# A conditioned decoder layer on one core: a new order for its opening

## The chip, the cores and the metric

The kernel runs on one core of a Trainium2 chip. The core has TensorE (PE, matrix products into PSUM; PEld is its weight load), VectorE (DVE), ScalarE (ACT), GpSimd (POOL) and SyncE (SP). SP, ScalarE and GpSimd each issue transfers, which run on 16 shared DMA engines. The metric is the device time of one execution in microseconds (us); smaller is better.

## The reference

One layer over x of 256 rows by 2048, in f32. A vector c of 2048 conditions it: nine rows of shifts, scales and gates come from `silu(c) @ w_ada + b_ada`.

```
c_act = silu(c)
mod = (c_act @ w_ada + b_ada).reshape(9, 2048)
h = rms_norm(x, norm_ffn1) * (1 + mod[1]) + mod[0]
x = x + 0.5 * mod[2] * swiglu(h, w_ffn1_gu, w_ffn1_down)     # w_gu: 2048 x 11264
h = rms_norm(x, norm_mix) * (1 + mod[4]) + mod[3]
x = x + mod[5] * token_mixing(h)                             # retention and windowed attention
h = rms_norm(x, norm_ffn2) * (1 + mod[7]) + mod[6]
x = x + 0.5 * mod[8] * swiglu(h, w_ffn2_gu, w_ffn2_down)
out = rms_norm(x, norm_final)
```

The change touches the first three lines and the beginning of the first `swiglu`.

## The kernel before

Everything is cut into tiles of 128 partitions. x lies in two row tiles t = 0 and 1 (`x_sb`); the 2048 columns are 16 blocks k of 128. To keep f32 accuracy at the speed of the rounded product type, every operand is split into a rounded part and the rest: ScalarE casts (`wh`, `hh`), VectorE subtracts (`wl`, `hl`), and `products` (lines 320 to 329) makes three matmuls of 512 columns for each k and t: `hh·wh`, `hl·wh`, `hh·wl`.

**The condition.** w_ada comes transposed, one row of 128 x 2048 (1 MB) for each mod index m and block k. `cact` holds silu(c) on every partition: c is loaded as one row (line 146), four matmuls with a column of ones spread it, and ScalarE applies Silu to each quarter (lines 168 to 171). `ada_pass` (line 204) multiplies half a row with half of `cact` and sums along it on VectorE; `ada_end` (221 to 224) adds the two halves and applies bias and gain. The gains and biases are loaded as short rows by `small_loads` (150 to 157, six transfers on SP, the identity among them) and turned into columns by three transposes in `columns_in` (175 to 188).

**The opening.** `place(m, k)` loads a w_ada row. The rows of k = 0 use two of the four `raw` buffers; all later rows take turns on a ring of two halves of one big tile, so the third row on the ring can be loaded only when the first has been passed. x's mean squares are summed on ScalarE in four parts a row tile (line 462, into the two `pd` banks, whose content nobody reads); `inv_rms` (474 to 488) makes 1/rms with a square root on ScalarE and six small VectorE operations. Block k of h is x times 1/rms (787), transposed on TensorE (788), modulated (497), and split (502, 503).

**The first products.** The first 12 column blocks n of w_gu are worked on while the condition is still being made: k comes in groups of 2, 3, 3, 4 and 4 blocks, and for each group all 12 n are visited (`visit`): load the k rows of block n into a `raw`, split, multiply. Between the groups the sums go to SBUF (`to_parts`, lines 835 and 837). During the visits of one group the rows of the next are loaded, passed, and made into h (`group`), a step at a time.

**What sets the order.** On SP the order is the program's, always. On the other engines a planner orders the instructions by its own estimate of when each can start, but for stretches under `manual_schedule(engines=ORDERED)`, where TensorE, VectorE and ScalarE also follow the program. Before the change only the ends of the three long products have such a stretch; the opening is the planner's. A DMA on SP uses one of eight semaphores in turn. In the planner's order, GpSimd's first transfers are the table of cosines and masks (879) and the sinks (880), though the program has them after the first FFN.

The opening's SP order is c, row (1,0), x tile 0, x tile 1, six small loads, row (0,0), rows (1,1) and (0,1), then w_gu blocks.

Of the kernel before, what the change touches and what calls it, by code (L numbers as in the profile page):

```python
# [17 lines left out]
P = 128  # L18
# [59 lines left out]
def layer_kernel(  # L78
# [38 lines left out]
    def nm(s):  # L117
        uid[0] += 1
        return f"{s}_{uid[0]}"
# [30 lines left out]
    def small_loads():  # L150
        nc.sync.dma_start(ident, consts[:, C_ID : C_ID + P])
        for i, src in enumerate((norm_ffn1, norm_mix, norm_ffn2)):
            nc.sync.dma_start(
                rows[i * KD : (i + 1) * KD, :P], src[0].rearrange("(k p) -> k p", p=P)
            )
        nc.sync.dma_start(rows[:, P : 2 * P], b_rows[:P])
        nc.sync.dma_start(rows[: 9 * KD - P, 2 * P : 3 * P], b_rows[P:])
# [10 lines left out]
    for j in range(D // CH):  # L168
        pt = acc_bank()
        nc.tensor.matmul(pt, ones, c_row[:, j * CH : (j + 1) * CH], start=True, stop=True)  # L170
        nc.scalar.activation(cact[:, j * CH : (j + 1) * CH], pt, AF.Silu)
# [108 lines left out]
    def gate_load(row, m):  # L280
        nc.gpsimd.dma_start(row, gate_d[m // 3][None, :].broadcast_to([P, D]))
# [186 lines left out]
    def inv_rms(ssq, t):  # L468
# [6 lines left out]
            out=s, in_=ssq[:, t * 4 : (t + 1) * 4], axis=AX.X, op=ALU.add  # L475
# [15 lines left out]
    def modulated(held, k, src, m_shift, act=False):  # L491

        h = t512()[:, :S]
        scale = modc[:, m_shift + 1, k : k + 1]
        shift = modc[:, m_shift, k : k + 1]
        if act:
            nc.scalar.activation(h, src, AF.Identity, bias=shift, scale=scale)
        else:
            nc.vector.tensor_scalar(
                out=h, in0=src, scalar1=scale, scalar2=shift, op0=ALU.mult, op1=ALU.add  # L500
            )
        nc.scalar.copy(held.hi[:, k, :], h)
        nc.vector.tensor_sub(held.lo[:, k, :], h, held.hi[:, k, :].bitcast(F32))  # L503
# [255 lines left out]

    place(1, 0)  # L760
    for t in range(NT):
        nc.sync.dma_start(x_sb[:, t, :], x[0, t * P : (t + 1) * P, :])
    small_loads()
    place(0, 0)
    place(1, 1)
    place(0, 1)
    columns_in()

    def group(ks):

        for k in ks:
            for m in (1, 0):
# [4 lines left out]
                if ks[0] == 0:  # L777
                    ada_end(m, slice(k, k + 1), early[m], 0 if m else None, passes)
                yield
        if ks[0] > 0:  # L780
            for m in (1, 0):
                ada_end(m, slice(ks[0], ks[-1] + 1), early[m], 0 if m else None, passes)
# [9 lines left out]
    for t in range(NT):  # L792
        for ci in range(4):
            square_sum(
                ssq[:, t * 4 + ci : t * 4 + ci + 1], x_sb[:, t, ci * CH : (ci + 1) * CH]
            )
    r = [inv_rms(ssq, t) for t in range(NT)]
    bounds = (0, 2, 5, 8, 12, 16)
    groups = [range(a, b) for a, b in zip(bounds, bounds[1:])]


    banks, moved = {}, set()
    chunks = list(range(2 * EARLY))

    def load_blocks(n, ks):
        raw = raws.tile([P, KB, CH], F32, tag="raw", name=nm("raw"))
        c0 = (n % 2) * DFF + (n // 2) * CH
        nc.sync.dma_start(
            raw[:, : len(ks), :],
            gu[ks[0] * P : (ks[-1] + 1) * P, c0 : c0 + CH].rearrange("(k p) n -> p k n", p=P),  # L810
        )
        return raw
# [27 lines left out]
    for _ in group(groups[0]):  # L840
        pass
    for g, ks in enumerate(groups):
# [5 lines left out]
        for i, n in enumerate(order):  # L848
            visit(n, ks, load_blocks(n, ks), n not in stay)
# [16 lines left out]
    gate_load(gate, 2)  # L866
# [12 lines left out]
    nc.gpsimd.dma_start(small_c[:, C_COS:], consts[:, C_COS:C_DEC])  # L879
    nc.gpsimd.dma_start(sink_b, sinks.broadcast_to([P, QH]))  # L880
# [369 lines left out]
```

## Time and profile before

| | us |
|---|---|
| median of 3 runs | 2430.84 (2430.41 to 2431.67) |
| profiled execution, first to last instruction | 2429.6 |
| first product of TensorE (spreading c) | 2.60 |
| first pass over a w_ada row | 7.02 |
| first product with w_gu | 26.57 |
| TensorE busy in the whole span | 2385.2 |

The profiled execution's own time is given as its span alone, 2429.6; the median of the runs is 1.2 above it. A row of the timeline reads: start, duration, engine, line of the kernel, operation, tile written <- tiles read, shapes, count, and in brackets the idle time before it with what ended it. An engine name with q (SPq) is its sequencer issuing a transfer. A row of the stage table reads: stretch, length, then busy time and number of instructions for each engine, the granted TensorE clock, the mean busy share of the DMA engines, and GB/s. A transfer's row gives its size and the time from issue to landing. A waits row gives the whole time, the number of times and the longest.

### The profile page before, as it was taken

The page shows a single profiled execution, that of the slowest core. Times are in us where ns is not written, and L with a number is a line of the kernel's source. Part 1 is how long each engine was busy: PE and PEld are TensorE (multiplying, and loading weights), DVE is VectorE, ACT ScalarE, POOL GpSimd, SP SyncE. Part 2 cuts the span into 40 slices and gives each one's busy share as a digit, 9 for nine tenths or more (in the row PEclk, how much of TensorE's full clock was granted, in tenths as well). Part 3 has the DMA queues.
Part 4 walks back from the last instruction along what each step waited for, and adds up shares of the span by engine and source line. Part 5 has one row for each costly group of instructions (what it writes and reads, how often), then busy time and mean ns, then how long its engine had stood idle before and what let it go on. Part 6 is the DMA issues. An engine that isn't in the chain of part 4 may idle for free. (4 is left out here: it accounts for less than half of the span.)

```text
span 2429.6 us, 29064 instructions
## 1 busy us (share of the span) xinstructions
PE 2385.2 (98%) x10798; PEld 1946.8 (80%) x10798; DVE 1701.3 (70%) x2735; ACT 1236.0 (51%) x1696; POOL 5.7 (0%) x14
## 2 busy tenths in 40 slices
PE   7999999999999999999999999999999999999998
PEld 4778888888787777788888888887788888888886
DVE  6998777778877677886666776767655555555656
ACT  6544545454545455554544444446554555554544
POOL 0000000000000000000000000000000000000000
PEclk9999999999999999999999999999999999999999
DMA  9987689998875665566676777755677777775563
GB/s 347 341 333 284 217 313 318 356 319 295 311 264 186 243 222 204 206 219 216 233 266 245 251 260 260 279 189 190 215 249 237 243 251 238 248 237 192 185 198 122
DMA packets 274545, 606.43 MB, mean 250 GB/s; under 512 B 40098, under 2 KB 40482, under 8 KB 255586
## 3 DMA queue, kind: packets, MB, share of 16 engines
q1 hardware_dynamic: 272898, 597.91, 70.8%
q0 software_dynamic: 928, 5.61, 0.6%
q8 instruction: 85, 1.39, 0.2%
q10 hardware_dynamic: 576, 1.05, 0.1%
q14 instruction: 58, 0.47, 0.1%
HBM read 595.06 MB, written 2.12 MB: 246 GB/s over the span
## 5 line engine op out<-in xcount | busy, mean ns | idle before, releaser
L336 DVE TENSOR_TENSOR wl<-raw,wh 128x1024 fp32r<-128x1024 f32 (+1 forms) x828 | 995.9, 1208 | 591.2 <-ACT wh L335 585.3
L335 ACT CAST wh<-raw 128x1024 fp32r<-128x1024 f32 (+1 forms) x828 | 861.4, 1042 | 973.0 <-PE pa L328 936.8
L327 PE MATMUL pa<-wh,hh 128*128 128x512 f32 x2224 | 870.5, 393 | 3.4 <-ACT wh L335 2.9
L328 PE MATMUL pa<-wh,hl 128*128 128x512 f32 x2224 | 869.9, 391 | 2.2 <-DVE hl L503 1.8
L329 PE MATMUL pa<-wl,hh 128*128 128x512 f32 x2224 | 798.0, 392 | 4.0 <-DVE wl L336 4.0
L327 PEld LDWEIGHTS pa<-wh,hh 128*128 128x128 f32 x2224 | 418.1, 188 | 93.4 <-ACT wh L335 4.4
L329 PEld LDWEIGHTS pa<-wl,hh 128*128 128x128 f32 x2224 | 415.9, 188 | 95.9 <-DVE wl L336 9.8
L328 PEld LDWEIGHTS pa<-wh,hl 128*128 128x128 f32 x2224 | 418.3, 188 | 89.8 <-DVE hl L503 2.5
L328 PE MATMUL pa<-wh,a 128*128 128x512 f32 x992 | 383.9, 389 | 0.0
L327 PE MATMUL pa<-wh,a 128*128 128x512 f32 x992 | 367.1, 390 | 1.6 <-DVE t L546 1.2
L329 PE MATMUL pa<-wl,a 128*128 128x512 f32 x992 | 367.1, 390 | 0.8 <-DVE wl L336 0.8
L327 PEld LDWEIGHTS pa<-wh,a 128*128 128x128 f32 x992 | 186.1, 188 | 41.5 <-DVE t L546 1.9
L329 PEld LDWEIGHTS pa<-wl,a 128*128 128x128 f32 x992 | 185.9, 188 | 40.6 <-DVE wl L336 2.4
L328 PEld LDWEIGHTS pa<-wh,a 128*128 128x128 f32 x992 | 186.3, 188 | 38.5
L204 DVE CUSTOM_DVE_ANT_0 slot<-slot,cact 128x512 f32<-128x512 f32 (+1 forms) x252 | 192.8, 814 | 10.5 <-DMA slot<-in_w_ada_dram 10.3
L204 DVE CUSTOM_DVE_ANT_0 raw<-raw,cact 128x512 f32<-128x512 f32 (+1 forms) x260 | 167.1, 696 | 42.5 <-DMA raw<-in_w_ada_dram 32.3
L368 DVE TENSOR_TENSOR a<-slot,a 128x512 fp32r<-128x512 f32 x124 | 85.0, 686 | 13.2 <-ACT a L367 13.2
L367 ACT CAST a<-slot 128x512 fp32r<-128x512 f32 x124 | 76.4, 616 | 14.8 <-PE pa L329 14.7
L442 ACT COPY slot<-a 128x512 uint16<-128x512 uint16 x54 | 38.5, 772 | 31.3 <-DMA a<-a 31.3
L204 DVE DVE_READ_ACCUMULATOR2_ANT sums<- 128x1 f32 x512 | 42.4, 83 | 0.0
L418 ACT COPY slot<-ps 128x512 f32<-128x512 f32 x52 | 29.4, 584 | 23.7 <-PE ps L417 23.5
L462 ACT ACTIVATE pd<-x_sb 128x512 f32<-128x512 f32 x32 | 19.0, 593 | 34.6 <-DVE x_sb L547 32.1
(164 smaller groups left out, 1024.2 us busy)
## 6 DMA issues: line engine op xcount, KB each, us to landing
raw<-in_w_ffn_gu_dram SPq DMA_DIRECT2D x152, 1024.0 KB, 5.2
raw<-in_w_in_dram SPq DMA_DIRECT2D x104, 1024.0 KB, 5.0
raw<-in_w_ffn_down_dram SPq DMA_DIRECT2D x88, 1024.0 KB, 5.1
slot<-in_w_ada_dram SPq DMA_DIRECT2D x76, 1024.0 KB, 7.3
raw<-in_w_ada_dram SPq DMA_DIRECT2D x64, 1024.0 KB, 4.8
raw<-in_w_ffn_gu_dram SPq DMA_DIRECT2D x24, 768.0 KB, 6.9
raw<-in_w_swa_branch_dram SPq DMA_DIRECT2D x16, 1024.0 KB, 5.3
raw<-in_w_ret_branch_dram SPq DMA_DIRECT2D x16, 1024.0 KB, 5.1
```

What stands on the lines that cost most here:

```text
L204: nc.vector.tensor_tensor_reduce(out=w[:, at], in0=w[:, at], in1=cact[:, at], scale=1.0, scalar=0.0, op0=ALU.mult, op1=ALU.add, accum_out= ...
L327: nc.tensor.matmul(ps, ah[:, j, ts], wh[:, j, :], start=first, stop=False)
L328: nc.tensor.matmul(ps, al[:, j, ts], wh[:, j, :], start=False, stop=False)
L329: nc.tensor.matmul(ps, ah[:, j, ts], wl[:, j, :], start=False, stop=last)
L335: nc.scalar.copy(hi, src)
L336: nc.vector.tensor_sub(lo, src, hi.bitcast(F32))
L367: nc.scalar.copy(hi, v)
L368: nc.vector.tensor_sub(lo, v, hi.bitcast(F32))
L418: nc.any.tensor_copy(dest, ps[:, : n * P])
L442: nc.any.tensor_copy(into[:, :, :, i], turned[:, i])
L462: nc.scalar.activation(side_bank(), src, AF.Square, accum_out=dest)
```

## The change

1. c: half of `cact` is loaded straight from DRAM, the row read once for each of 128 partitions (512 KB on SP), and gets one Silu in place; the other half is spread by two matmuls as before.
2. The six small loads go from SP to GpSimd. The table of cosines and masks and the sinks are held behind the first gate load, so they no longer run in the opening.
3. x comes in halves of 1024 columns, and SP's order is c, half of c, row (1,0), x tile 0, row (0,0), w_gu block 0, x tile 1, rows (1,1) and (0,1), w_gu block 1.
4. The squares of x: two quarters on ScalarE, the far half in one operation on VectorE.
5. Group 0 and the visits of blocks 0 and 1 in it are written out by hand in an ordered stretch: k = 0 first and apart from k = 1, row tile 0 of it before row tile 1, with half-width splits.
6. In three places `warm` puts 6, 4 and 6 matmuls of the identity with 512 columns of x on TensorE; their result is not read.

```diff
     def small_loads():
-        nc.sync.dma_start(ident, consts[:, C_ID : C_ID + P])
+        nc.gpsimd.dma_start(ident, consts[:, C_ID : C_ID + P])
...
-    for j in range(D // CH):
+    near = cact[:, : D // 2]
+    nc.sync.dma_start(near, c[:, : D // 2].broadcast_to([P, D // 2]))
+    small_loads()
+    nc.scalar.activation(near, near, AF.Silu)
+    for j in range(D // CH // 2, D // CH):
...
+    def x_load(t):
+        for i in range(2):
+            at = slice(i * D // 2, (i + 1) * D // 2)
+            nc.sync.dma_start(x_sb[:, t, at], x[0, t * P : (t + 1) * P, at])
...
     place(1, 0)
-    for t in range(NT):
-        nc.sync.dma_start(x_sb[:, t, :], x[0, t * P : (t + 1) * P, :])
-    small_loads()
+    x_load(0)
     place(0, 0)
+    first_two = [load_blocks(0, groups[0])]
+    x_load(1)
     place(1, 1)
     place(0, 1)
-    columns_in()
+    first_two.append(load_blocks(1, groups[0]))
...
+    def far_squares(t):
+        far = x_sb[:, t, D // 2 :]
+        nc.vector.tensor_tensor_reduce(
+            out=junk, in0=far, in1=far, scale=1.0, scalar=0.0,
+            op0=ALU.mult, op1=ALU.add,
+            accum_out=ssq[:, t * 4 + 2 : t * 4 + 3],
+        )
...
+    def warm(n):
+        idle = side_bank()
+        for _ in range(n):
+            nc.tensor.matmul(idle, ident, x_sb[:, 0, :CH], start=True, stop=True)
...
-    for _ in group(groups[0]):
-        pass
+    T = [slice(t * P, (t + 1) * P) for t in range(NT)]
+    with tc.manual_schedule(engines=ORDERED):
+        first_pass(1, 0, 0)
+        first_pass(1, 0, 1)
+        root_table()
+        columns_in()
+        first_end(1, 0)
+        near_squares(0)
+        warm(6)
+        far_squares(0)
+        r.append(inv_rms(ssq, 0, 3))
+        ps = bank()
+        first_turn(ps, 0, 0)
+        first_pass(0, 0, 0)
+        first_pass(0, 0, 1)
+        first_end(0, 0)
+        modulated(held, 0, ps[:, T[0]], 0, act=True, ts=T[0])
+        banks[0] = [acc_bank() for _ in range(NT)]
+        w00 = first_split(0, 0)
+        first_products(0, 0, 0, w00)
+        w01 = first_split(0, 1)
+        near_squares(1)
+        warm(4)
+        far_squares(1)
+        r.append(inv_rms(ssq, 1, 3))
+        first_turn(ps, 0, 1)
+        modulated(held, 0, ps[:, T[1]], 0, act=True, ts=T[1])
+        first_products(0, 0, 1, w00)
+        ps = bank()
+        for t in range(NT):
+            first_turn(ps, 1, t)
+        warm(6)
+        for m in (1, 0):
+            first_pass(m, 1, 0)
+            first_pass(m, 1, 1)
+            first_end(m, 1)
+        banks[1] = [acc_bank() for _ in range(NT)]
+        w10 = first_split(1, 0)
+        for t in range(NT):
+            first_products(1, 0, t, w10)
+        modulated(held, 1, ps[:, :S], 0, act=True)
+        w11 = first_split(1, 1)
+        for n, piece in ((0, w01), (1, w11)):
+            for t in range(NT):
+                first_products(n, 1, t, piece)
...
         for i, n in enumerate(order):
-            visit(n, ks, load_blocks(n, ks), n not in stay)
+            if g > 0 or n > 1:
+                visit(n, ks, load_blocks(n, ks), n not in stay)
...
+    with tc.issue_after(gate_loaded.ins):
+        nc.gpsimd.dma_start(small_c[:, C_COS:], consts[:, C_COS:C_DEC])
+        nc.gpsimd.dma_start(sink_b, sinks.broadcast_to([P, QH]))
```

`first_pass` is `ada_pass` on half a row, `first_end` `ada_end` for one k, `first_turn` the scaling and transpose of one block of one row tile, `first_split` `split` of one k of w_gu block 0 or 1 (512 columns), `first_products` the three matmuls for one block, k and t, `near_squares` two `square_sum` calls.

85 lines of the change are left out of this document (54 added, 31 removed).

## The prediction

> **What bounds the kernel now.** I read the head of the page first, then the busy time by stage, then the opening instruction by instruction, then the transfers.
>
> ```profile
> span 2429.6 us, 29064 instructions
> PE 2385.2 (98%) x10798; PEld 1946.8 (80%) x10798; DVE 1701.3 (70%) x2735; ACT 1236.0 (51%) x1696; POOL 5.7 (0%) x14
> ```
>
> The span lies 1.2 us under the 2430.84 us median of the runs; I add 1.2 to what I work out for it. TensorE is busy almost throughout, so this edit can win or lose only where TensorE waits or runs slowly.
>
> ```profile
> core 0: us, PE busy (x) PEld busy (x) DVE busy (x) ACT busy (x) POOL busy (x), PEclk, DMA share, GB/s
> 0.00:33.00 33.00, 16.27 (x33) 8.85 (x34) 18.68 (x54) 17.03 (x37) 1.42 (x6) 1.00 0.93 331
> 33.00:60.00 27.00, 25.81 (x111) 20.09 (x110) 22.24 (x35) 19.77 (x30) 0.00 (x0) 1.00 1.00 368
> 60.00:100.00 40.00, 40.00 (x180) 32.96 (x180) 36.15 (x53) 21.88 (x35) 0.00 (x0) 1.00 0.95 357
> 100.00:180.00 80.00, 75.44 (x326) 58.25 (x325) 74.89 (x122) 39.05 (x62) 0.00 (x0) 1.00 0.87 325
> 432.00:446.00 14.00, 14.00 (x63) 11.62 (x62) 9.46 (x16) 7.36 (x9) 0.56 (x1) 1.00 1.01 401
> ```
>
> TensorE idles in the first 33 us, hardly from 33 to 60 (there the transfers are full, share 1.00), and 4.6 us of 100 to 180, where VectorE is at 74.89 of 80. So a lead won in the opening must also be a lead of the transfers and of VectorE, or it is given back before 180.
>
> ```profile
> 4.68 0.60 ACT L171 ACTIVATE cact<-pa 128x512 f32<-128x512 f32 x1 [2.66 <-PE pa L170]
> 6.39 0.60 ACT L171 ACTIVATE cact<-pa 128x512 f32<-128x512 f32 x1 [1.11 <-PE pa L170]
> 2.60 7.16 PE L170 MATMUL pa<-c_row,t 1*128 1x512 f32 x8 [2.60 <-DMA c_row<-in_c_dram]
> 8.71 0.31 SPq L157 DMA_DIRECT2D t<-in_b_ada_dram  x1
> 11.81 0.58 ACT L171 ACTIVATE cact<-pa 128x512 f32<-128x512 f32 x1
> 12.42 1.22 DVE L204 CUSTOM_DVE_ANT_0 raw<-raw,cact 128x1024 f32<-128x1024 f32 x1 [4.17 <-ACT cact L171]
> 23.04 0.34 SPq L199 DMA_DIRECT2D slot<-in_w_ada_dram  x1
> 26.57 0.80 PE L327 MATMUL pa<-wh,hh 128*128 128x512 f32 x1 [0.81 <-ACT wh L335]
> 32.20 0.62 PE L329 MATMUL pa<-wl,hh 128*128 128x512 f32 x2
> 33.12 0.39 PE L328 MATMUL pa<-wh,hl 128*128 128x512 f32 x1
> 34.94 0.39 PE L327 MATMUL pa<-wh,hh 128*128 128x512 f32 x1
> ```
>
> The reader is to see three things. The second pass over the first w_ada row waited until 12.42 because the last quarter of c stood behind the squares of x on ScalarE (11.81). The products of the first two blocks begin at 26.57 and ran slowly until 32.20; from 33.12 to 34.94 eight go out, 0.227 each. The one at 34.94 is the first of block 2, so by then the 24 products of blocks 0 and 1 were out. And the row load of the next group leaves at 23.04, when the last pass over row (1,1) has freed its half of the ring; two gu loads stand behind it on SP.
>
> **The change, part by part.** *The c half and the first pass.* Two of four c products go (the four ran 7.16 in all, and ScalarE's Silu after one and the next stand 1.71 apart, 4.68 and 6.39: 1.71 each), and a 512 KB load comes.
>
> ```profile
> raw<-in_w_ada_dram SPq DMA_DIRECT2D x1, 512.0 KB, 3.6
> GB/s 0 9 47 309 382 393 330 51 140 426 431 421 440 421 330 382 262 169 351 253 234 281 417 417 407 414 396 410 398 461 412 382 384 384 419 417 440 372 391 426
> row<-gate_d POOLq DMA_DIRECT2D x3, 1024.0 KB, 6.7
> dec<-in_consts_dram POOLq DMA_DIRECT2D x1, 1024.0 KB, 5.1
> sink_b<-in_sinks_dram POOLq DMA_DIRECT2D x1, 16.0 KB, 7.3
> gate_d<-t POOLq DMA_DIRECT2D x3, 8.0 KB, 3.1
> ```
>
> The load takes the place on SP from which 512 KB landed in 3.6 (issued 1.14): 4.7. That every partition reads the same row of c has no price of its own in sight: a gate row spread so landed in 6.7 beside other traffic, a plain 1 MB in 5.1. The second row shows the first 35 us in 40 slices of 0.875: there the queue runs at 421 to 440 GB/s when nothing stalls it, 1.25 us for 512 KB. In the new SP order, with 0.4 for the small loads and no stall, that lands w_ada (1,0) at 7.6, x half 0 of tile 0 at 8.9, its other half at 10.1, (0,0) at 12.6, gu block 0 at 13.9, x tile 1 at 16.4, (1,1) at 18.9, (0,1) at 21.4, gu block 1 at 22.7. The dip to 51 and 140 lies between sink_b's issue and its landing, and I put it down to its 128-byte pieces; they leave the opening. VectorE's two passes over (1,0) end near 8.9 instead of 13.6.
>
> *Small loads on GpSimd.* SP loses six issues, and the wait of 3.1 before 8.71. On GpSimd they follow one another from 1.3 at 0.5 to 0.7 apiece; the last leaves near 4.1 and lands between 7.2 (by gate_d's 3.1) and 11.4 (by sink_b's 7.3). I take 8.5: 16 rows of 512 bytes are nearest to gate_d. What waits is the transposes of columns_in, and VectorE behind them is free only at 8.9: cost nothing up to there, then one for one.
>
> *The unread products.* Sixteen f32 products of 512 columns.
>
> ```profile
> 1083.27 0.60 PE L1061 MATMUL pd<-slot 128*128 128x256 f32 x2
> 1083.70 0.38 PE L1064 MATMUL pd<-slot 128*128 128x128 f32 x2
> 15.86 0.21 DVE L185 COPY gains<-ps 128x48 f32<-128x48 f32 x1 [1.26 <-PE ps L180]
> 16.76 0.29 ACT L477 ACTIVATE rs<-sum,eps 128x1 f32<-128x1 f32 x1
> 17.09 0.16 DVE L481 RECIPROCAL rs<-rs 128x1 f32<-128x1 f32 x1 [0.44 <-ACT rs L477]
> 20.55 0.47 PE L788 MATMUL ps<-small_c,t 128*128 128x128 f32 x1 [4.72 <-ACT t L787]
> 24.08 0.56 ACT L497 ACTIVATE t<-ps,modc 128x256 f32<-128x256 f32 x1 [0.56 <-PE ps L788]
> 25.13 0.40 ACT L502 CAST hh<-t 128x256 fp32r<-128x256 f32 x1
> 67.87 0.62 ACT L335 CAST wh<-raw 128x512 fp32r<-128x512 f32 x1
> ```
>
> A 256-column f32 product took 0.43 at full speed (1083.27 to 1083.70), so 512 columns take 0.86, and 1.71 slowly. In the trace the speed doubled 5.6 after the products began (26.57 to 32.20). The first six can start when x half 0 is there and columns_in is through, 9.2: slowly to 14.8 (3.3 of them), then 2.7 at 0.86: TensorE is free at 17.2. [...]
>
> *The written chain.* VectorE: columns_in and first_end to 10.3 (copies of 0.21 and the like from 15.86 on, about 0.8, then three of about 0.16), square sum of the far half to 11.4 (as wide as a pass, 1.22, of which the next hides 0.08), the root chain 1.3 (ScalarE's 0.29 with the 0.33 from 16.76 to 17.09, and five small ones of 0.16 with their hand-overs), so the first r is used at 12.8; passes over (0,0) to 15.5. The transposes of row tile 0 could then run, but stand behind the unread products: 17.2, which costs 1.7. From there each step waits for the last: transpose 17.7 (0.47), modulate and cast at half their widths 18.4 (under 0.56 and 0.40), the two half-width splits of gu block 0 on ScalarE to 19.5 (0.62, the second hidden in part), the two near squares of tile 1 to 20.7, VectorE's far half 20.2 to 21.4, root and scale 23.1; the four unread products began after the first of those squares, 20.1, and end 23.5; transpose, modulate, cast, subtract: 24.9. Only now come the passes over (1,1): 24.9 to 27.3, and over (0,1) to 30.4 with their ends. The last six unread products, 25.8 to 31.0, run under them and cost nothing. wl of block 1 is ready at 31.0; six products, 32.4; the k = 1 halves of h and wl by 32.5; twelve products of 0.227: 35.1. Against 34.94 that is nothing won on TensorE: the earlier start and the higher clock are spent on the order.
>
> *SP behind it.* The row load of group 1 needs the ring half of (1,1): 27.4 instead of 23.04, with the queue empty since 22.7.
>
> ```profile
> slot<-in_w_ada_dram SPq DMA_DIRECT2D x1, 1024.0 KB, 6.3
> raw<-in_w_ffn_gu_dram SPq DMA_DIRECT2D x2, 512.0 KB, 7.7
> raw<-in_w_ffn_gu_dram SPq DMA_DIRECT2D x1, 512.0 KB, 8.0
> 58.54 0.50 PE L327 MATMUL pa<-wh,hh 128*128 128x512 f32 x1 [0.94 <-ACT wh L335]
> 32.32 1.22 DVE L336 TENSOR_TENSOR wl<-raw,wh 128x1024 fp32r<-128x1024 f32 x1
> ```
>
> Before, that row landed 6.3 after 23.04, at 29.3, and the gu pair behind it near 30.7 and 32.0. On an empty queue 512 KB took 3.6, so 1 MB about 4.8: 32.2, and the stream is 2.8 late; were it to start at once, 27.4 plus 2.5, 0.5 late. At 58.54 TensorE waited for the cast of a gu load (issued 48.8, landed 8.0 later), so up to there the transfers are the limit and the lag comes through. VectorE has done two row passes less than at 33.5 before (end of the subtraction at 32.32), 2.3 late; the two lags run side by side, the larger counts. I take 2.5 of a possible 0.2 (TensorE's own lag) to 2.8.
>
> *The constants.* The table and sink loads move behind the first gate row, near 433. There TensorE is busy 14.00 of 14 us beside a full queue, and SP waits for buffers:
>
> ```profile
> SPq L312 <- DVE wl L336: 66.9, 16, 6.2
> ```
>
> that is 66.9 of the 100 us from 400 on, so loads run ahead of use: nothing, up to 1 if sink_b's dip (about 1.7 us at 51 and 140 GB/s) repeats. The one square sum less per tile on ScalarE is paid by the pass-wide one on VectorE, counted above; the narrower root chain, slices and ends alter only widths that stand in the chain. Sum: 2429.6 + 0.2 to 2.8, taken 2.5, is 2432.1, with 1.2 around it 2433.3.
>
> **The rivals.** *Absorbed:* the lag is made up, since raws are four deep and 60 to 100 shows no idle TensorE; 2431 give or take 1. For it speaks the SP wait for buffers later on, against it the wait at 58.54.
>
> *Faster:* the unread products end before 15.5 and gate nothing. Then data decide: far half of x tile 1 at 16.4, passes over (1,1) from 20.6 to 22.9, end of the 24 products 30.7, 4.2 sooner, and the row load no later than before. That alone is 2426.6, within the bound; with part of the 4.6 us of TensorE's idle time in 100 to 180 gone too, since a new start gives the scheduler another order, 2424. Against it: six products need 10.3 at the slow and 5.2 at the full rate, and the rate begins slow.
>
> *Slower, by the clock:* the unread products do not raise the rate, as the c products did not. Then six end at 19.5, the four run 22.5 to 29.3, the last six 31.6 to 41.9, and 18 products, slow at first, end near 49: 14 late, 2445. It decides if the rate has not doubled by the end of the first six. For it only the c products, one row deep, speak.
>
> *Slower, by the small loads:* they land by sink_b's 7.3, at 11.4, so columns_in and all behind it move 2.5: 5.0 in all, 2435.8. The point is a landing at 11.3. sink_b's pieces were 128 bytes, these are 512, against it; the shared engines are as full, for it.
>
> **How the numbers follow.** Differences under 0.2% (4.9 us) count as no change here. Likeliest, the late stream at 2433.3 (2430 to 2435.7): 0.34, and Absorbed 0.20, both no change: 0.54. Faster past the bound 0.17. Slower by the clock 0.10, by the small loads or more such lateness 0.19: 0.29. The range leaves out the far part of the faster case and of the clock case: 2425.5 to 2440.
>
> **What would show it.** The first pass ends near 7.3 and the second near 8.9; the first six unread products end near 17.2 with the rate doubling among them; (1,1) is passed near 25 to 27; a hole in the transfers follows gu block 1 from about 22.7 to 29; block 2's first product comes at 35.1 or later; a longer wait near 58. The forecast is wrong if the rate stays slow, if row (1,1) is passed before 23, or if VectorE's waits between 100 and 180 change by more than some 3 us.

## The result and the profile after

The changed kernel takes 2442.68 us (2439.35 to 2442.9), the kernel before 2431.26 (2430.41 to 2432.78) on the same chip: a ratio of 1.0041, with a 95% interval of 1.0029 to 1.0053. It is 11.4 us slower. The prediction was 2433.3 with a range up to 2440, and no change as the likeliest outcome.

The profiled execution is the quickest of the changed kernel's: 2439.35, 1.8 over its span. The lag that the trace shows, 7.9, is therefore 3.3 short of that of the other executions, and of those 3.3 there is no trace. The head of the page after, and one of its rows of transfer queues:

```profile
span 2437.5 us, 29136 instructions
PE 2398.4 (98%) x10826; PEld 1951.0 (80%) x10826; DVE 1704.8 (70%) x2742; ACT 1233.9 (51%) x1693; POOL 8.7 (0%) x20
...
q8 instruction: 85, 1.39, 0.2%
```

There are 28 matmul records more: an f32 product appears as two (the first six unread ones as x12 below), so sixteen unread products are 32, and two products of c are gone. The last row has no part in the prediction, and turned out to matter. Busy time by stage (us from and to, length, busy time of each engine, granted clock, share of the transfers, GB/s):

```profile
0.00:33.00 33.00, 23.90 (x51) 10.29 (x52) 18.60 (x54) 14.36 (x30) 3.38 (x10) 1.00 0.76 273
33.00:60.00 27.00, 24.68 (x109) 19.83 (x108) 22.38 (x34) 19.04 (x30) 0.00 (x0) 1.00 1.03 401
60.00:100.00 40.00, 39.01 (x173) 31.49 (x173) 35.65 (x54) 23.23 (x37) 0.00 (x0) 1.00 0.96 354
100.00:180.00 80.00, 76.36 (x328) 58.95 (x327) 75.32 (x121) 38.26 (x59) 0.00 (x0) 1.00 0.87 325
560.00:720.00 160.00, 156.48 (x677) 127.32 (x676) 129.95 (x233) 76.84 (x93) 0.00 (x0) 0.99 0.81 296
```

TensorE is busier in the first 33 us, by the unread products, while the transfers carry less (share 0.76, before 0.93). From 33 to 100 it has 2.1 us of new idle time. And from 560 to 720, far behind the change, it is busy 156.48 where it was 158.40 before:

```profile
560.00:720.00 160.00, 158.40 (x697) 130.09 (x696) 132.90 (x237) 78.71 (x95) 0.00 (x0) 1.00 0.82 298
```

I followed the lag by counting the matmuls of weights in the order of time, and comparing the start of the n-th one in two traces. Counted from 0, number 24 is the first of block 2; the last column is the last one of all. First row: starts in the kernel before; below, starts minus these, in us. The names are those of the experiments below.

```
n                            0      6     12     24     36     72    600   2250   2500   2681   2950   last
before                   26.57  29.72  32.20  34.94  37.66  46.08 178.11 559.85 616.65 660.00 720.97 2419.3
after                    -5.97   2.57   2.00   4.54   4.54   4.28   3.55   3.73   5.16   7.90   8.30   8.24
e1_no_unread             -7.85  -3.59   0.83   4.19   4.23   3.97   3.49   3.55   3.41   4.09   4.09   3.77
f1_no_unread_quarter     -7.86  -3.62   0.80   4.46   4.89   4.63   3.55   3.67   6.35   9.14   9.17   9.33
e5_tiny_unread           -8.00  -1.18   0.68   2.12   2.12   2.01   0.41   1.77   3.99   5.72   6.48   6.84
e7_no_last_six           -6.17  -0.68   4.36   8.12   8.16   7.89   7.24   7.37   8.63  10.91  10.91  11.79
e8_wider_ring            -7.77  -3.52   0.91   4.63   5.12   4.85   4.99   5.02   5.58   5.59   5.63   5.86
g1_second_passes_behind  -6.18   2.37   1.80   1.90   2.94   4.27   3.35   3.51   4.87   7.45   7.80   7.72
h2_changed_wider_ring    -6.04   2.50   1.93   3.82   4.31   4.05   3.41   3.58   5.70   8.06   8.82   8.79
g2_changed_whole         -5.96   2.59   2.03   4.39   4.39   4.13   5.45   5.44   5.39   5.39   5.41   5.53
f3_before_quarter        -0.27  -0.27  -1.04  -1.05  -1.05  -1.05  -2.24  -2.17  -0.86   1.98   2.42   2.32
f4_before_half            0.15   0.15  -0.14  -0.15  -0.15  -0.14  -1.11   0.03   0.02   0.07   0.07  -0.29
e6_rows_early_no_unread  -7.76   1.54   3.19   4.66   4.66   4.40   2.96   3.76   3.62   3.64   8.70   8.66
e2_constants_late        -0.56  -0.57  -0.59  -0.54  -0.54  -0.80  -0.51  -0.51  -0.65  -0.63   1.50   1.19
g4_before_half_spread    -0.36  -0.37  -0.29  -0.21  -0.21  -0.20  -1.42  -1.43  -1.38   0.21   0.20   0.24
```

So there are two losses. The opening starts 6 us ahead, is 4.5 behind at block 2, and keeps 3.5 to 3.7 until 560. Then 4.6 more are lost between 560 and 720, in the down product of the first FFN, where no line of the change does anything and TensorE, VectorE and ScalarE have the same order as before. The opening after, instruction by instruction (start, duration, engine, operation, idle time before it):

```profile
7.93 1.22 DVE L208 CUSTOM_DVE_ANT_0 raw<-raw,cact 128x1024 f32<-128x1024 f32 x1 [6.91 <-DMA raw<-in_w_ada_dram]
9.61 1.23 DVE L208 CUSTOM_DVE_ANT_0 raw<-raw,cact 128x1024 f32<-128x1024 f32 x1 [0.45 <-DMA raw<-in_w_ada_dram]
...
11.55 7.54 PE L846 MATMUL pd<-x_sb,small_c 128*128 128x512 f32 x12 [0.71 <-ACT pd L466]
...
15.92 0.19 PEld L846 LDWEIGHTS pd<-x_sb,small_c 128*128 128x128 f32 x1 [0.45 <-issue]
...
18.92 0.27 PE L841 MATMUL ps<-small_c,t 128*128 128x128 f32 x1
20.59 0.50 PE L331 MATMUL pa<-wh,hh 128*128 128x512 f32 x1 [1.40 <-ACT wh L339]
...
26.61 1.22 DVE L208 CUSTOM_DVE_ANT_0 slot<-slot,cact 128x1024 f32<-128x1024 f32 x1
...
27.53 5.32 PE L846 MATMUL pd<-x_sb,small_c 128*128 128x512 f32 x12
...
29.01 0.33 SPq L203 DMA_DIRECT2D slot<-in_w_ada_dram  x1
...
32.29 0.79 PE L331 MATMUL pa<-wh,hh 128*128 128x512 f32 x1
...
34.04 1.23 DVE L208 CUSTOM_DVE_ANT_0 slot<-slot,cact 128x1024 f32<-128x1024 f32 x1 [1.19 <-DMA slot<-in_w_ada_dram]
...
36.34 0.42 DVE L507 TENSOR_TENSOR hl<-t,hh 128x256 fp32r<-128x256 f32 x1
...
36.81 0.50 PE L332 MATMUL pa<-wh,hl 128*128 128x512 f32 x1 [2.13 <-DVE hl L507]
```

The reader is to see four things. The steps come in the forecast order, each 1 to 2 us later. The unread products raised the rate (their records start 0.85 apart up to 15.9 and 0.43 from there: doubled 4.4 after the start). The last six keep TensorE until 32.29. And VectorE waits 1.19 for the late row (1,2), passes over it until 36.3, and only then makes the k = 1 half of hl, which had its input at 33.8 (the cast of hh ran from 33.38 for 0.39); TensorE waits 2.13 for it.

### The profile page after: what moved, and what is told of

The parts are those of the page before. It is cut to its first block, busy times and chain, and to the rows that moved or that the text cites. A ratio compares the mean times of both kernels' runs of the same rounds, so it can differ in the third digit from the quotient of the medians.

```text
span 2437.5 us, 29136 instructions
## 1 busy us (share of the span) xinstructions
PE 2398.4 (98%) x10826; PEld 1951.0 (80%) x10826; DVE 1704.8 (70%) x2742; ACT 1233.9 (51%) x1693; POOL 8.7 (0%) x20
## 4 chain that ended last, share of the span: by engine, by line
PE 88%; DVE 4%; issue 1%; ACT 1%; DMA 1%; SPq 0%; DVEq 0%; ACTq 0%
PE pa L333 28%; PE pa L332 28%; PE pa L331 28%; DVE wl L340 1%; PE ps L421 1%; DVE slot L208 1%; DMA slot<-in_w_ada_dram 1%; DVE t L533 0%; DVE slot L886 0%; PE pd L1017 0%; ACT wh L339 0%; PE pd L1013 0%; PE ps L1086 0%; ACT hh L542 0%; ACT t L531 0%
## 5 line engine op out<-in xcount | busy, mean ns | idle before, releaser
L446 ACT COPY slot<-a 128x512 uint16<-128x512 uint16 x54 | 38.4, 771 | 27.4 <-DMA a<-a 27.4
L886 DVE TENSOR_TENSOR slot<-slot,pa 128x512 f32<-128x512 f32 x56 | 35.7, 678 | 0.0
```

The costliest lines, as they stand in the source:

```text
L446: nc.any.tensor_copy(into[:, :, :, i], turned[:, i])
L886: nc.vector.tensor_add(p, p, b)
```

## The experiments

Where nothing else is said, an experiment's edit is made on the changed kernel. The kernel before ran beside each and took 2431.7 to 2431.9.

### The unread products: time, or number?

**e1_no_unread:** the unread products go.

```
-        warm(6)
...
-        warm(4)
...
-        warm(6)
```

> The changed kernel without its sixteen unread products, all else the same. If the unread products hold the chain up (the transpose of row tile 0 stood behind them until 18.9, while VectorE was ready at 17.4), the first row load of group 1 leaves about 1.5 to 2 us sooner than 29.0, at about 27, but the first 24 products run at the slow rate, 0.43 each, for the first 5 us, so that the first product of block 2 comes within 2 us of the changed kernel's; the whole time is 2441 to 2444. If the unread products are worth what they were put in for, it is 3 us or more above the changed kernel. If they are the cause of the loss, it falls by 5 us or more, to under 2438.

Measured: 2435.19 (2432.62 to 2436.03), ratio 1.0013 (1.0003 to 1.0022). The unread products cost 7.5. But at block 2 the lag is the same without them (4.19 against 4.54). What is missing is the loss from 560 on, in a stretch in which the order of every engine is the same in both kernels.

**e5_tiny_unread:** the same products, 16 columns wide.

```
-            nc.tensor.matmul(idle, ident, x_sb[:, 0, :CH], start=True, stop=True)
+            nc.tensor.matmul(idle[:, :16], ident, x_sb[:, 0, :16], start=True, stop=True)
```

> The changed kernel with the sixteen unread products cut from 512 to 16 columns: the same instructions in the same places on every engine, but nearly no TensorE time. Theory 'their time': what the unread products cost (2442.7 against 2435.2 without them) is the TensorE time in front of the products that are read, so it goes with their width: 2435 (2433.5 to 2437), opening lag 3.5 to 4.2 at 50 us as without them, and no further lag between 560 and 720 us. Rival 'their number': it is the sixteen more instructions, which move every later one in the instruction stream and in its loading: 2440 to 2443, with the 3 to 5 us lost between 560 and 720 us again.

Measured: 2439.37 (2437.89 to 2440.93), ratio 1.0032 (1.002 to 1.0044), between the spans of the two theories. The traced execution is the quickest of its six; in it the opening is the better one, 2.1 behind at block 2. The loss behind 560 is back, 4.7 us of it, though the products now take nearly no time; f1 below tests whether it comes with their number alone. In this trace the read products take their full rate at 34.4:

```profile
32.89 0.78 PE L331 MATMUL pa<-wh,hh 128*128 128x512 f32 x1
34.42 0.50 PE L332 MATMUL pa<-wh,hl 128*128 128x512 f32 x1 [0.76 <-DVE hl L507]
34.75 0.39 PE L333 MATMUL pa<-wl,hh 128*128 128x512 f32 x1
34.98 0.40 PE L331 MATMUL pa<-wh,hh 128*128 128x512 f32 x1
```

and without any unread products only at 38.6:

```profile
38.13 0.63 PE L331 MATMUL pa<-wh,hh 128*128 128x512 f32 x1
38.55 0.50 PE L332 MATMUL pa<-wh,hl 128*128 128x512 f32 x1
38.89 0.39 PE L333 MATMUL pa<-wl,hh 128*128 128x512 f32 x1
```

This does not show that products of 16 columns raise the rate. In the traces of f2, g3 and h1 below, which have the same products, the full rate came at 39.7, 37.6 and 36.7, and in e1, f1, e6 and e8, which have none, between 37.1 and 40.2. So the small opening lag of e5 was in part luck of that execution.

**f1_no_unread_quarter:** e1, with 32 products of one row and 16 columns in TensorE's idle time ahead of c's first product.

```
+    bits = ones.bitcast(mybir.dt.bfloat16)[:, :P]
...
+        for _ in range(32 if j == D // CH // 2 else 0):
+            nc.tensor.matmul(pt[:, :16], bits, bits[:, :16], start=True, stop=True)
```

> The changed kernel without its unread products (2435.2), and 32 products of one row and 16 columns, of constants, right at the start, where TensorE has nothing to do: as many TensorE instructions as the unread products were (each of those appears twice in the trace), and no time. TensorE's instructions come in pieces of 16 KB, some 127.5 matmuls and their weight loads apiece, so 32 more bring every later piece a quarter of one earlier, some 7 us. Theory 'the pieces': where the pieces fall among the row loads decides over the loss between 560 and 720 us: it comes back, 2438 to 2442, with the opening lag of 3.5 to 4.5 unchanged. Rival 'the unread products, not their number': no loss there, 2434.5 to 2436.5.

Measured: 2440.48 (2439.65 to 2441.28), ratio 1.0037 (1.0024 to 1.005): 5.3 slower than e1, with the same lag up to 560 (3.67 against 3.55) and 5.5 more at 720. Products that take no time that counts and change no order cost 5.3 us, half a millisecond later. VectorE's wait for the w_ada rows from 560 to 725, in e1 and then in f1 (us in total, times, longest):

```profile
DVE slot L208 <- DMA slot<-in_w_ada_dram: 4.9, 8, 1.2
```

```profile
DVE slot L211 <- DMA slot<-in_w_ada_dram: 13.3, 9, 4.0
```

In e1 TensorE is fully busy from 560 to 640, in f1 it is not:

```profile
560.00:640.00 80.00, 80.00 (x354) 66.25 (x353) 65.86 (x119) 39.20 (x45) 0.00 (x0) 1.00 0.86 317
```

```profile
560.00:640.00 80.00, 77.16 (x337) 62.54 (x336) 63.01 (x117) 36.67 (x42) 0.00 (x0) 1.00 0.82 308
```

What moves with the number is the q8 row of the page, the queue that the trace calls instruction: in the changed kernel 85 transfers of 16 KB, one for each 28.7 us of the span and for some 127 matmuls and their weight loads (10,826 of each). The row names no engine. I take the pieces for TensorE's own instructions, loaded during the run, since they move with TensorE's count: in e1 they came at 536, 565, 594 and 625 us, in f1, with 32 products more, 3 to 5 us earlier, at 531, 561, 591 and 620. In the changed kernel's trace a piece held its transfer engine for 1.03 us in the median (0.88 to 1.79). The w_ada row issued near 525.9 landed at 532.9 in e1 and at 534.4 in f1, where the piece of 531 came while it ran; the row issued near 555.9 landed at 563.0 and, with the piece of 561 in it, at 564.4. In e1 these two pieces came 3 and 2 us after those rows had landed. Two of the steps of the loss are so seen with their piece. A third (a row issued near 571 took 1.5 longer) has none beside it; I take it for a consequence of the first two, which is not shown. All twenty traces together bear the delay out. Of the w_ada rows issued between 500 and 725, 41 had a piece begin 1.0 to 6.3 us after their issue (a span chosen on these traces): none landed in under 8.0 us, and their median is 8.6. Of the 267 that had no piece beside them, 207 landed in under 8.0, with a median of 7.3; the other 60 took longer, for a reason that was not shown.

**f2_tiny_unread_whole** and **g2_changed_whole:** one whole piece, 128 matmuls, more than e1. e5 and the changed kernel each get 96 one-row products, 32 where f1 has them and 64 ahead of columns_in.

```
+        idle = side_bank()
+        for _ in range(64):
+            nc.tensor.matmul(idle[:, :16], bits, bits[:, :16], start=True, stop=True)
         root_table()
         columns_in()
```

> The changed kernel with the unread products cut to 16 columns (2439.4, opening lag 0.4 to 1.8, 5 us lost between 560 and 720), and 96 one-row products of 16 columns more, so that all that was added is one whole piece of 16 KB and the later pieces fall where they fell without any. Theory 'the pieces': the loss between 560 and 720 goes, the small opening lag stays: 2431.5 to 2435. Rival 'not the pieces': 2438 to 2441.

> The changed kernel with 96 one-row products of 16 columns, 32 ahead of c's products and 64 behind them, so that its TensorE instructions stand a whole piece of 16 KB later than without the unread products. Theory 'the pieces': the loss between 560 and 720 us goes and the opening lag stays at 3.5 to 5: 2435.5 to 2438.5. Rival 'the changed kernel loses it whatever the pieces': 2441 to 2444.

Measured: f2 2436.74 (2434.86 to 2440.08), ratio 1.002 (1.001 to 1.0029); g2 2438.87 (2435.79 to 2439.45), ratio 1.0024 (1.0014 to 1.0035). In both traces the loss behind 560 is gone (g2: 5.44 before it, 5.41 after it). Both medians lie above the span expected, since the opening came out worse: f2 is 5.2 behind at block 2, as its far half of x tile 0 landed 1.3 later, and g2 loses 1.3 more between 100 and 140, where its rate was halved for a while (granted clock 0.83 from 120 to 130, 1.00 in the changed kernel). The runs of g2 fall into two groups, three at 2435.8 to 2436.7, the traced one among them, and four at 2438.9 to 2439.5; of the slower group there is no trace. The page of g2, with 96 products more than the changed kernel, counts one piece more:

```profile
q8 instruction: 86, 1.41, 0.2%
```

**f3_before_quarter, f4_before_half, g4_before_half_spread:** the kernel before, with 32, 64, and 24 + 40 one-row products (these 40 behind c's third product).

```
+        for _ in range(32 if j == 0 else 0):
+            nc.tensor.matmul(pt[:, :16], bits, bits[:, :16], start=True, stop=True)
         nc.tensor.matmul(pt, ones, c_row[:, j * CH : (j + 1) * CH], start=True, stop=True)
```

> The kernel before with 32 products of one row and 16 columns at its start, and nothing else. Theory 'the pieces': a shift of a quarter of a piece alone moves the time of the kernel before too, by 1 to 5 us, up or down: 2433 to 2436 if it meets the conditioning rows as it did in the changed kernel. Rival 'the changed order is needed': 2431 to 2432.5, as before.

> The same with 64 such products, half a piece, of which some 30 can run before c's products and the rest hold these back by about 2 us. Theory 'the pieces': another time again, between 2428 and 2437, with lag or lead arising in steps of 1 to 2 us where a row load lands late or early for the same issue. Rival: 2431 to 2433.5, a constant lag of at most 2 from the start on.

> The kernel before with half a piece again (f4_before_half gave 2430.2 against 2431.8), with 24 of the 64 products ahead of c's first product and 40 behind its last, so that they hold nothing back. Theory 'the place of the pieces alone': 2429 to 2430.5, as fast or a little faster than f4_before_half. Rival 'an accident of that run': 2431.5 to 2433.

Measured: f3 2435.14 (2432.68 to 2436.7), ratio 1.0013 (1.0003 to 1.0022); f4 2430.23 (2429.01 to 2431.96), 0.9993 (0.9984 to 1.0003); g4 2429.94 (2429.23 to 2431.78), 0.9994 (0.9985 to 1.0003). The new order is not needed: a quarter of a piece alone costs the kernel before 3.3, with 4.6 lost between 560 and 720 (-2.17 to 2.42). Half a piece gave 1.6 and 1.9 less than before in two placements; both intervals hold 1.

One step of this loss is TensorE's rate. At 657 it waits for t; the changed kernel first, then e1:

```profile
659.22 0.50 PE L331 MATMUL pa<-wh,a 128*128 128x512 f32 x1 [1.75 <-DVE t L550]
...
660.95 1.22 PE L333 MATMUL pa<-wl,a 128*128 128x512 f32 x2 [0.40 <-DVE wl L340]
661.97 0.63 PE L331 MATMUL pa<-wh,a 128*128 128x512 f32 x1
```

```profile
657.02 0.50 PE L331 MATMUL pa<-wh,a 128*128 128x512 f32 x1 [1.57 <-DVE t L550]
...
658.75 0.73 PE L333 MATMUL pa<-wl,a 128*128 128x512 f32 x2 [0.40 <-DVE wl L340]
```

After a wait of 1.75 the products run at half rate for 3.4 us, with a granted clock of 0.62 from 660 to 664; after one of 1.57 they do not. Such a half rate costs some 1.7 us (half of 3.4) on top of the late rows. f1 (1.80) and f3 (2.09) show it too, g2 and the kernel before (1.21 each) do not. But the length of the wait does not decide alone: g4 waits 1.21 and 0.40 at this place, as the kernel before does, and its products run at half rate from 653.4 to 656.8; that is about as much as the 1.6 that its row in the table loses between 560 and 720. What decides beside it was not shown.

### The opening

**e3_rows_early** and **e6_rows_early_no_unread:** row (1,1) is passed ahead of tile 1's squares, with and without the unread products.

```
+        first_pass(1, 1, 0)
+        first_pass(1, 1, 1)
+        first_end(1, 1)
         near_squares(1)
...
-        for m in (1, 0):
-            first_pass(m, 1, 0)
-            first_pass(m, 1, 1)
-            first_end(m, 1)
+        first_pass(0, 1, 0)
+        first_pass(0, 1, 1)
+        first_end(0, 1)
```

> The changed kernel with the passes over row (1,1) put before the squares of x tile 1, so that its half of the ring comes free sooner; the passes over (0,1) stay where they are. If the late row load makes the opening's lag, it leaves at about 24.5 instead of 29.0, the stream's hole shrinks by about 4 us, and the lag at 40 us falls from 4.5 to 2 or less; the whole time falls by at least 2.5, to 2440 or less. If the lag is TensorE's own (the chain of row tile 1), the passes only push that chain 2 us back and the time is the changed kernel's or up to 2 more.

> Row (1,1) passed before tile 1's squares, as in e3_rows_early (2441.4, lag 8.5 us at 70 us), and without the unread products. Theory 'lateness': a stream that is late by more than some 4 us meets the conditioning rows of the first down product badly and loses 3 to 5 us more between 560 and 720 us, whatever made it late; then this kernel, if its opening lag is over 4, loses them too: 2438 to 2442. Rival 'the unread products': the loss between 560 and 720 us comes with them alone; then no further lag there, and the end is the opening lag and no more: 2434 to 2438.

Measured: e3 2441.45 (2440.84 to 2443.81), ratio 1.0041 (1.0026 to 1.0056), 9.6 behind at block 2; e6 2437.11 (2435.16 to 2439.81), ratio 1.0021 (1.0011 to 1.0031), 4.7 behind at block 2. The row load of group 1 did leave earlier, at 24.4 in e3 and 22.4 in e6 (29.0 in the changed kernel, 27.0 in e1). An earlier row load buys nothing if tile 1's chain pays for it. The profiled execution of e6 is the slowest of its nine; it lost 5 between 660 and 720 with e1's number of instructions, so the number is not the only thing that brings a loss on there. What differs in this stretch is the planner's order: in e6 VectorE passes over a late row ahead of a `wl` that TensorE waits for, and after the wait the rate is halved as well (granted clock 0.50 from 674 to 676). First e6, then e1, where this `wl` is the second of two made ahead of the passes:

```profile
668.87 0.69 DVE L208 CUSTOM_DVE_ANT_0 slot<-slot,cact 128x512 f32<-128x512 f32 x1 [2.37 <-DMA slot<-in_w_ada_dram]
...
671.32 1.22 DVE L340 TENSOR_TENSOR wl<-raw,wh 128x1024 fp32r<-128x1024 f32 x1
...
672.60 0.73 PE L333 MATMUL pa<-wl,a 128*128 128x512 f32 x2 [3.13 <-DVE wl L340]
```

```profile
665.76 2.35 DVE L340 TENSOR_TENSOR wl<-raw,wh 128x1024 fp32r<-128x1024 f32 x2
...
668.63 0.68 DVE L208 CUSTOM_DVE_ANT_0 slot<-slot,cact 128x512 f32<-128x512 f32 x1
```

Of the twenty kernels only e6 and e2 have another order from 560 to 720 than the kernel before. No run changes this order by itself.

**e7_no_last_six:** the first ten unread products stay.

```
             first_turn(ps, 1, t)
-        warm(6)
         for m in (1, 0):
```

> The changed kernel without the last six unread products alone (the first six and the four stay). In the changed kernel the last six ran from 27.5 to 32.3, past the moment when the weights of block 1 were there. Theory 'the last six stand in the way': the products of block 1 start at about 30.5 instead of 32.3; the lag at 50 us falls from 4.5 to 3 to 4; 2435 to 2440. Rival 'they only keep the clock up': without them the products run slowly after 30 us, and the lag stays at 4.5 or rises: 2442 or more.

Measured: 2441.7 (2440.86 to 2442.8), ratio 1.0043 (1.0028 to 1.0058). The rival's mechanism is in the trace: the products start earlier (-0.68 at n = 6 instead of 2.57) and then run at the low rate, 8.1 behind at block 2. But the traced execution is the slowest of its four, and the median is 1.0 below the changed kernel's and under the rival's 2442. With twelve of TensorE's records fewer, the pieces are moved too (3.5 lost between 560 and 720 instead of 4.6). Whether the last six earn more by the rate than they cost is therefore not shown.

**g1_second_passes_behind:** the passes over row (1,2) come last in the written order, behind hl and wl.

```
                 first_products(n, 1, t, piece)
+        second = group(groups[1])
+        next(second)
+        second = chain((None,), second)
...
-        coming = iter(()) if final else group(groups[g + 1])
+        coming = iter(()) if final else group(groups[g + 1]) if g else second
```

> The changed kernel (2442.7) with one move on VectorE: the two passes over row (1,2), which ran from 34.0 to 36.3 after 1.2 us of waiting for that row, come behind the k = 1 half of hl and the wl of block 1 that the products wait for; order and number of all else stay. Theory 'VectorE's order in the opening': TensorE's wait of 2.1 us for hl at 36.8 goes, hl is there at 34; the lag at 40 us falls from 4.5 to 2 to 3, and 1.5 to 2 us of it last: 2440 to 2441.5. Rival 'the late row load': the row passes, and with them the transfers behind, become 0.9 us later, the lag at 60 us is 4 as before: 2442 to 2444.

Measured: 2440.45 (2438.76 to 2440.87), ratio 1.0034 (1.0022 to 1.0046). The wait of 2.13 is gone and the lag at block 2 falls from 4.54 to 1.90; but at n = 72 it is 4.27 again. TensorE, and before it ScalarE's cast, then waits for a gu load:

```profile
45.81 0.39 PE L333 MATMUL pa<-wl,hh 128*128 128x512 f32 x1
...
47.13 0.50 PE L331 MATMUL pa<-wh,hh 128*128 128x512 f32 x1 [0.94 <-ACT wh L339]
```

**e8_wider_ring** (on e1) and **h2_changed_wider_ring** (on the changed kernel): rows (1,2) and (0,2) get buffers of their own, so that the row load of group 1 waits for no pass.

```
             rows_of[m, k] = raw_row()
+        elif k == 2:
+            rows_of[m, k] = part[2 - m][:, :D]
         else:
```

> The changed kernel without unread products (2435.2), and rows (1,2) and (0,2) in buffers of their own, so that the row loads of group 1 wait for no pass and leave right behind gu block 1, near 15 to 18 us instead of 27.0. Theory 'the late row load sets the lag': the hole in the transfers from 25 to 30 us goes, and the lag at 50 us falls from 4.0 to under 2: 2431.5 to 2433.5. Rival 'VectorE sets it': the passes over group 1 cannot start before 31 us anyway, VectorE's work in the opening being in one chain; the lag stays 3 to 4: 2434.5 to 2436.

> The changed kernel with rows (1,2) and (0,2) in buffers of their own, so that the row loads of group 1 wait for no pass; the passes over row (1,2) thereby stand behind the second half of hl and the wl of block 1, and the planner's order differs from there to about 100 us. Theory 'two limits side by side': g1 alone won 1.6 at 40 us and lost it to a late gu load at 45.8; e8 filled the hole in the transfers and lost to a slow TensorE. Here both go and the clock is up, so the lag at 60 us falls from 4.5 to under 2.5 and stays: 2438 to 2440.5 with the loss between 560 and 720 us, 2434 to 2436 if the new order escapes it. Rival 'neither is the limit': lag 3.5 to 5 at 60 us, 2441 to 2444.

Measured: e8 2436.42 (2435.48 to 2438.26), ratio 1.002 (1.0011 to 1.003); h2 2440.88 (2439.84 to 2441.91), ratio 1.0039 (1.0023 to 1.0054), between the two spans expected; its lag at n = 72, 4.05, is the rival's. The hole in the transfers from 24 to 32 is there in the changed kernel, and gone in e8 (a share of 1.02) and in h2. The changed kernel first, then h2:

```profile
24.00:32.00 8.00, 7.12 (x21) 3.42 (x20) 5.81 (x16) 2.26 (x6) 0.00 (x0) 1.00 0.26 73
32.00:60.00 28.00, 25.68 (x111) 20.31 (x111) 23.19 (x37) 19.71 (x31) 0.00 (x0) 1.00 1.03 401
```

```profile
24.00:32.00 8.00, 7.12 (x21) 3.38 (x20) 5.81 (x15) 2.27 (x6) 0.00 (x0) 1.00 1.01 401
32.00:60.00 28.00, 26.12 (x112) 20.34 (x111) 23.37 (x36) 19.91 (x31) 0.00 (x0) 1.00 0.84 301
```

A share of 1.01 there instead of 0.26, and yet the same lag: the stream then stops behind it (0.84), because the gu buffers are not free before TensorE has used them. In h2 the row passes also stand behind hl, and the lag at n = 18 is 2.0; then ScalarE's four copies of finished sums stand ahead of the cast for block 2:

```profile
35.12 2.64 ACT L890 COPY slot<-pa 128x512 f32<-128x512 f32 x4 [0.89 <-PE pa L333]
37.65 2.00 ACT L339 CAST wh<-raw 128x1024 fp32r<-128x1024 f32 x2
```

By these traces three limits lie within 2 us of each other, the late stream, VectorE's order and ScalarE's order, and taking away one or two brings up the third. No run moved ScalarE's copies, so the third is read from the trace and not tested.

### Loads and constants, and all together

**e2_constants_late:** the kernel before, with table and sinks behind the gate row only. **e4_loads_only:** the same with the half of c by transfer and the small loads on GpSimd as well, in the kernel before's order.

```
-    nc.gpsimd.dma_start(small_c[:, C_COS:], consts[:, C_COS:C_DEC])
-    nc.gpsimd.dma_start(sink_b, sinks.broadcast_to([P, QH]))
+    with tc.issue_after(gate_loaded.ins):
+        nc.gpsimd.dma_start(small_c[:, C_COS:], consts[:, C_COS:C_DEC])
+        nc.gpsimd.dma_start(sink_b, sinks.broadcast_to([P, QH]))
```

> The kernel before with one thing changed: the loads of the table and of the sinks go behind the first gate row. If the loss behind 540 us (4 us in the profiled run, in the down product of the first FFN) comes from these loads being moved, this run shows it alone: 4 us or more above before, 2435 or more, and VectorE's waits for w_ada rows between 560 and 720 as long as in the changed kernel (10 us instead of 5). If that loss follows from the opening's lag, this run is at 2431 give or take 1.5, or up to 2 below it, since the opening is freed of the dip to 51 GB/s.

> The kernel before with the loads of the change alone: half of c spread by transfer, the small loads on GpSimd, the constants behind the gate row; x, the rows, and the planner's order of the opening as before, no unread products. If the loads are good and the written order loses, the first passes are done by 9.5 instead of 13.6, the first product of TensorE with w_gu comes 2 to 3 us before 26.57, and the whole time is 2427 to 2430. If moving loads to GpSimd or spreading c by transfer is itself harmful, it is above 2432.

Measured: e2 2433.02 (2430.35 to 2434.22), ratio 1.0003 (0.9994 to 1.0013); e4 2433.19 (2431.61 to 2435.38), ratio 1.0006 (0.9997 to 1.0016). Neither can be told from no change. In e2's trace 2.1 are lost between 660 and 720, with the order of the planner that e6 has there (TensorE waits 1.66 for that `wl`), so e2 does not differ from the kernel before by the loads alone. e4's first product comes 2.35 later than before: without the new order the loads alone win nothing.

**g3_tiny_behind_half:** e5 with g1's move and f1's 32 products, together half a piece. **h1_tiny_ring_half:** e5 with the wider ring and the 32 products.

> The unread products cut to 16 columns (opening lag 0.4 to 1.8), the passes over row (1,2) behind hl and wl, and 32 one-row products more, which makes half a piece of 16 KB. Both theories added: opening lag from -1 to 1, no loss between 560 and 720 us as with half a piece on the kernel before: 2429.5 to 2432.5, level with the kernel before or a little ahead. Rival 'the new order has its own worst place': 2433.5 to 2440.

> The same wider ring, the unread products cut to 16 columns, and 32 one-row products more (half a piece of 16 KB): all that won before, together. Theory: opening lag of 0 or a lead of up to 2 us at 60, no loss between 560 and 720: 2429 to 2432. Rival 'each order has its own places where the pieces hurt': 2433 to 2438.

Measured: g3 2433.39 (2431.51 to 2433.99), ratio 1.0004 (0.9995 to 1.0013); h1 2434.71 (2433.11 to 2436.72), ratio 1.0011 (1.0002 to 1.002). Neither lost much between 560 and 720 (0.8 in g3, nothing in h1). g3 is 9.3 below the changed kernel and level with the kernel before. h1 misses what was expected of it: 4.7 behind at block 2, by the same copies ahead of the cast. No version tried beats the kernel before by more than its interval.

## Why the prediction was wrong, point by point

- **The unread products:** "run under them and cost nothing" for the last six, and 1.7 for the first. This is the step that failed most: without the sixteen the kernel takes 7.5 less (e1). They were costed by their time alone. Their number, 32 of TensorE's records, costs 5.3 by f1 against e1 (2440.48 and 2435.19), 3.3 in the kernel before (f3), and 3.8 in the changed kernel by g2; the prediction has no such term. Their width costs some 3.3 more (2442.68 against e5's 2439.37). That they raise the rate was right: it doubled 4.4 after their start, against the 5.6 taken from the trace before.
- **TensorE's own lag:** "0.2". Measured: 4.54 at block 2, 2.0 of it at n = 12, as the last six held TensorE to 32.29, and 2.5 by the wait for hl. (Without any unread products it is 4.19, in e1, whose products run at the low rate up to 38.6.) The prediction did not ask what else VectorE may put ahead of that half of hl. The written order binds only what is written in it, and the planner's passes over row (1,2) took the place.
- **SP behind it:** "27.4" for the row load. It left at 29.01, 1.6 later, since the first pass ended near 9.1 instead of 7.3 and the second near 10.8 instead of 8.9: the half of c landed at 5.7 and not at 4.7, the row behind it, for which the passes waited, at 9.5 and not at 7.6, and the small loads by 10.4 and not at 8.5. The hole in the transfers came (share 0.26 from 24 to 32).
- **The lag of the stream:** "taken 2.5" of 0.2 to 2.8. Measured 4.3 at n = 72, and 3.5 to 3.7 up to 560. The mechanism was there, and its size was wrong, by the 1.6 of the row load and the limits that stand beside it. By e8 and h2 it is not the only one.
- **The constants:** "nothing, up to 1". This holds by e2: the ratio's interval, 0.9994 to 1.0013, holds 1, with 1.3 between the medians, and e2's trace is 0.6 ahead up to 660, where the planner's other order begins. The same paragraph of the prediction speaks of one square sum less per tile on ScalarE; there are two less, four before and two after, which changes nothing in the sum.
- **The rivals:** "Slower by the clock" did not happen. "Slower by the small loads" was half right: they landed at 10.4, short of its point of 11.3. "Absorbed" failed, since the lag of the opening is still there at 560.
- **What stays open:** the 3.3 us by which the profiled execution was quicker than the others; whether each step of the loss between 560 and 720 is a piece of instructions in the way of a row, of which two were seen and followed; what delays the rows that are late with no piece beside them; and what decides, beside the length of a wait, whether the rate is halved.

## What to carry to other kernels

Here instructions that ran in idle time were not always free, in a stage that lives on loads landing just in time: 32 of them cost 5.3 us (f1 against e1, with the pieces of the instruction queue 3 to 5 us earlier) and 3.3 (f3), while 64 cost nothing (f4, g4). So when an edit changes the number of TensorE's instructions, add as many empty ones to the kernel before and compare with that. In an order written out by hand, check what the planner may still put between the written steps. And compare the planner's orders far behind an edit before comparing the times: in e2 and e6 another order there went with a loss of 2 and 5 us in the trace.

## What the runs showed of the hardware

- The queue that the trace calls instruction moved 85 pieces of 16 KB in the changed kernel's span of 2437.5, one for some 127 matmuls, and 86 with 96 products more (g2); a piece held its transfer engine for 1.03 us in the median of the changed kernel's trace. Two w_ada rows that ran beside a piece took 8.5 us in f1 and 7.0 and 7.1 without one in e1, and in all traces the 41 rows with a piece 1.0 to 6.3 us behind their issue took 8.0 us or more, against a median of 7.3 with none.
- A wait of 1.75 us with one of 0.40 behind it went with a half rate for 3.4 us (granted clock 0.62 from 660 to 664). Waits of 1.21 and 0.40 went with one in g4 and with none in the kernel before.
